# Weight sums of a fast FFN: three of four on VectorE from loaded blocks, and a later negation for the down sets

## The chip, the cores and the metric

The kernel runs on one core of one Trainium2 chip. The metric is device time in microseconds (us). Names in the profile: PE is TensorE (matmuls), PEld its weight loads, DVE is VectorE, ACT is ScalarE, POOL is GpSimd, SP is SyncE; a "q" behind a name (SPq, POOLq) is the engine's sequencer, which issues DMAs and waits.

## The reference, cut to what matters

The network is a trunk of two layers on 528 tokens (512 and 16 learned ones) with a width of 1024. Each layer is FFN, token mixer, FFN; the mixer is not touched here. All values are float32.

```python
def swiglu(x, w_gate, w_up, w_down):
    return (jax.nn.silu(x @ w_gate) * (x @ w_up)) @ w_down

for l in range(DEPTH):                      # DEPTH = 2
    h = h + 0.5 * swiglu(rmsnorm(h, norm_gains[l, 0]), ffn_w_gate[l, 0], ffn_w_up[l, 0], ffn_w_down[l, 0])
    h = h + mixer(rmsnorm(h, norm_gains[l, 1]), ...)
    h = h + 0.5 * swiglu(rmsnorm(h, norm_gains[l, 2]), ffn_w_gate[l, 1], ffn_w_up[l, 1], ffn_w_down[l, 1])
return rmsnorm(h, final_norm)[:, N_META:]
```

The four FFNs have a hidden width of 2816. Of the last one only 512 of the 528 tokens are needed.

## The kernel before, in words

**Seven products in place of eight.** A product of two matrices, each cut into 2 x 2 blocks, is made with seven block products instead of eight (Strassen's scheme in Winograd's form). The weights of a "set" are four blocks W11, W12, W21, W22 of 128 x 1024 floats (512 KB) in DRAM (`win`). Three products use a block as it is: "1" takes W11, "2" takes W12, "4" takes W22. The other four need sums of blocks:

- "7": S3 = W21 - W11
- "6": S2 = W22 + S3
- "5": S1 = W21 + W22
- "3": S4 = S2 - W12

An FFN has 15 sets: 11 pairs for gate and up (sets 0 to 10, each making 256 hidden columns of both), in groups of 4, 4 and 3, and four down sets (11 to 14, two behind each of the first two groups). The down product of the third group is made in the plain way. From one pair to the next the order of products interleaves: 1 of the next pair, 7 of this one, 2 of the next, 4 and 3 of this one, 6 and 5 of the next (`ffn_steps`). Behind a group of four its two down sets are worked off, and products 1, 2, 6, 5 of the next pair stand among their last products.

**hi and lo.** The weights go to PE in two parts: `hi`, a cast that ACT makes (L264), and `lo`, the rest, that DVE makes by subtracting `hi` (L265). A product is 24 matmuls of 264 columns (256 in the last FFN), about 2.9 us of PE. `make` runs three products ahead of use, `fetch` nine; `hi` and `lo` have four buffers each, and a cast waits until PE is done with the block four places before. Casts are queued behind the last snapshot (`W.behind`).

**Snapshots.** Products 1, 6 and 7 leave an intermediate state of a PSUM accumulator, which ACT copies out (L575, `c<-ss`), before the next product may add to that accumulator. Other PSUM reads are on DVE (L581, L591, L598 in the pairs, L693 in the down sets, where `h` is added to). In the down sets ACT and DVE also make the operands (L646, L647, L651).

**The weight sums.** `block` (L198) loads a block of `win` by SP's queue. `negative` (L203) is a copy with factor -1 on ACT, in the profile `s<-w`. `add` (L208) is a DMA of POOL's queue that adds to what is in the tile. Before the change a set gets:

- S3: negation of W11 (ACT), then the accumulating load of W21 from DRAM (POOL, `s<-win`)
- S2: load of W22 (SP), then the accumulating copy of S3 (POOL, `w<-s`)
- S1: load of W21 (SP), then the accumulating load of W22 (POOL, `w<-win`)
- S4: for pairs 0 and 1 the negation of W12 and an accumulating copy of S2 (`s<-w`); from set 2 on a subtraction on DVE (L233, `s<-w,w`), when the block of product 6 has been cast

All but S4 are traced in `fetch`, at the moment when block W11 is requested (in the opening two pairs of the first FFN, in `make`).

**Buffers.** Raw blocks have 3 buffers (`wraw`), S3 and S4 share 3 (`wsa`), S2 and S1 share 3 (`wsb`). A buffer is reused when its readers are done, so an instruction that writes it may wait in its queue.

**Order.** Each engine and each DMA queue works in order. The order is written by a planner at build time: it goes by the position in the program and by a model of when operands and buffers will be there. So an instruction whose data come later than modelled holds up what stands behind it in its queue.

## Time and profile before

| what | value |
|---|---|
| median of 3 runs | 2238.69 us (2238.67 to 2239.18) |
| profiled execution | 2233.24 us, of which span 2231.4 us |
| PE busy, weight loads busy | 2170.3 us (97%), 2075.3 us (93%) |
| DVE busy | 1700.7 us (76%) |
| ACT busy | 1244.2 us (56%) |
| POOL | 164.4 us (7%), nearly all of it the issue of 188 DMAs |
| granted PE clock, mean | 0.996 |
| DMA | 330.29 MB, mean 148 GB/s |

The four FFNs lie at about 7 to 370, 775 to 1130, 1130 to 1480 and 1860 to 2210 us of the span (a first product may start before the last down product of the FFN ahead ends); the mixers lie between. Rows are read like this: a group of instructions has line, engine, operation, out<-in by the program's names with the numbers left off, count, then busy time, mean ns of one, and idle time of the engine before them with what ended it. A wait row has engine, tile and line of who waits, then who ended the wait, then us in total, times, longest. A timeline row has start, duration, engine, line, operation, and in brackets the idle time before it and what ended that. The tile `w` is any block of `win`, `s` is S3 or S4, `ss` is PSUM.

### The profile page before, as it was taken

To read this page: it belongs to the slowest core of one execution; us is meant where nothing else is said; L and a number is where in the kernel's file an instruction comes from. 1 tells how busy PE (TensorE), PEld (TensorE's weight loads), DVE (VectorE), ACT (ScalarE), POOL (GpSimd) and SP (SyncE) were. 2 spreads that over 40 slices of the span, in tenths; PEclk is the share of its full clock that TensorE was granted. 3 is DMA by queue.
4 is the path that set the end of the run, shared out by engine and by line. 5 is a ranking of instruction groups with operands and counts; after the bars stand their busy time and mean duration, and the time that the engine had idled before them with its cause. 6 is when DMAs were issued, how large, how long until landed. Compare 5 with 4: busy or idle time off the path is not lost. (4 is left out here: it accounts for less than half of the span.)

```text
span 2231.4 us, 40120 instructions
## 1 busy us (share of the span) xinstructions
PE 2170.3 (97%) x16506; PEld 2075.3 (93%) x16506; DVE 1700.7 (76%) x2623; ACT 1244.2 (56%) x1815; POOL 164.4 (7%) x192
## 2 busy tenths in 40 slices
PE   7999999999999999999999999999999999999898
PEld 7999999989999999999999999999788888999897
DVE  8877877577876679687788778676779768687777
ACT  8555555345784555454675455553557836545553
POOL 1111100000000011111011111000000001111100
PEclk9999999999999999999999999999999999999999
DMA  9877753212114577777668777421111237677761
GB/s 280 226 190 203 198 150 109 77 48 72 43 39 133 133 189 191 211 203 190 179 166 212 190 208 202 139 100 67 57 67 57 88 104 199 177 200 191 187 180 67
DMA packets 92647, 330.29 MB, mean 148 GB/s; under 512 B 10288, under 2 KB 12720, under 8 KB 92464
## 3 DMA queue, kind: packets, MB, share of 16 engines
q1 hardware_dynamic: 63440, 226.65, 28.2%
q0 software_dynamic: 27072, 98.58, 24.4%
q8 instruction: 130, 2.13, 0.4%
q10 hardware_dynamic: 1952, 2.50, 0.4%
q14 instruction: 53, 0.43, 0.1%
HBM read 289.94 MB, written 2.10 MB: 131 GB/s over the span
## 5 line engine op out<-in xcount | busy, mean ns | idle before, releaser
L571 PE MATMUL ss<-xc,whi 128*128 128x264 f32 (+1 forms) x4928 | 909.2, 286 | 26.1 <-ACT c L575 16.5
L571 PEld LDWEIGHTS ss<-xc,whi 128*128 128x128 f32 x4928 | 768.8, 190 | 31.1 <-ACT c L575 18.8
L571 PE MATMUL ss<-xc,wlo 128*128 128x264 f32 (+1 forms) x2464 | 702.8, 285 | 2.7 <-DVE wlo L265 2.7
L265 DVE TENSOR_TENSOR wlo<-w,whi 128x1024 fp32r<-128x1024 f32 (+1 forms) x301 | 365.3, 1216 | 152.8 <-ACT whi L264 152.7
L571 PEld LDWEIGHTS ss<-xc,wlo 128*128 128x128 f32 x2464 | 467.4, 190 | 4.3 <-DVE wlo L265 4.3
L264 ACT CAST whi<-w 128x1024 fp32r<-128x1024 f32 (+1 forms) x301 | 312.1, 1048 | 136.2 <-PE ss L571 52.2
L438 PE MATMUL mm<-x,whi 128*128 128x264 f32 (+1 forms) x1712 | 384.8, 315 | 0.0
L438 PEld LDWEIGHTS mm<-x,whi 128*128 128x128 f32 x1712 | 278.4, 188 | 16.6 <-issue 1.0
L438 PE MATMUL mm<-x,wlo 128*128 128x264 f32 (+1 forms) x856 | 266.1, 315 | 0.0
L685 PE MATMUL ss<-g,whi 128*128 128x264 f32 (+1 forms) x1280 | 239.5, 285 | 4.4 <-DVE h L693 3.1
L264 ACT CAST whi<-raw 128x1024 fp32r<-128x1024 f32 x126 | 132.0, 1048 | 163.6 <-PE mm L438 102.8
L685 PEld LDWEIGHTS ss<-g,whi 128*128 128x128 f32 x1280 | 198.6, 188 | 7.0 <-ACT whi L264 3.4
L265 DVE TENSOR_TENSOR wlo<-raw,whi 128x1024 fp32r<-128x1024 f32 x126 | 153.9, 1221 | 59.3 <-ACT whi L264 58.4
L685 PE MATMUL ss<-g,wlo 128*128 128x264 f32 (+1 forms) x640 | 181.2, 283 | 0.0
L575 ACT COPY c<-ss 128x528 f32<-128x528 f32 (+1 forms) x132 | 78.3, 593 | 181.6 <-PE ss L571 181.4
L265 DVE TENSOR_TENSOR wlo<-s,whi 128x1024 fp32r<-128x1024 f32 x120 | 146.5, 1221 | 37.5 <-ACT whi L264 37.5
L438 PEld LDWEIGHTS mm<-x,wlo 128*128 128x128 f32 x856 | 159.6, 188 | 8.5 <-issue 0.7
L438 PE MATMUL ss<-g,whi 128*128 128x264 f32 (+2 forms) x900 | 166.2, 299 | 0.0
L438 PEld LDWEIGHTS ss<-g,whi 128*128 128x128 f32 x900 | 131.7, 188 | 5.3
L264 ACT CAST whi<-s 128x1024 fp32r<-128x1024 f32 x120 | 126.1, 1051 | 10.9 <-PE ss L571 7.2
L208 POOL DMA_DIRECT2D w<-win x60 | 54.5, 908 | 1029.3 <-DVE wlo L265 410.3
L203 ACT ACTIVATE s<-w 128x1024 f32<-128x1024 f32 x68 | 71.6, 1056 | 89.7 <-DMA w<-win 77.9
(265 smaller groups left out, 3405.4 us busy)
## 6 DMA issues: line engine op xcount, KB each, us to landing
w<-win SPq DMA_DIRECT2D x299, 512.0 KB, 5.4
raw<-wts SPq DMA_DIRECT2D x126, 512.0 KB, 3.2
s<-win POOLq DMA_DIRECT2D x60, 512.0 KB, 5.2
w<-s POOLq DMA_DIRECT2D x60, 512.0 KB, 5.5
w<-win POOLq DMA_DIRECT2D x60, 512.0 KB, 7.5
s<-w POOLq DMA_DIRECT2D x8, 512.0 KB, 8.4
h<-xt SPq DMA_DIRECT2D x3, 528.0 KB, 6.3
out<-h ACTq DMA_DIRECT2D x4, 256.0 KB, 2.4
```

What stands on the lines that cost most here:

```text
L203: self.nc.scalar.activation(t, w, AF.Copy, scale=-1.0)
L208: self.nc.gpsimd.dma_start(t, src, accum_op=ALU.add)
L264: nc.scalar.copy(hi[:, cs], w[:, cs])
L265: nc.vector.tensor_tensor(lo[:, cs], w[:, cs], hi[:, cs].bitcast(F32), ALU.subtract)
L438: TE.matmul(acc.half[i][:width], lhs, rhs[:, acc.spans[i]], start=first, stop=last)
L571: TE.matmul(acc[:, j], a[:, j, k], b[:, at], start=bool(begin and k == 0 and i == 0), stop=k == len(x) - 1 and i == 2, skip_group_check=no ...
L575: W.behind = S.copy(part(st, q), acc).ins
L685: TE.matmul(acc[:, j], a[:, j, k], xs[b][:, k], start=bool(begin and k == 0 and i == 0), stop=k == 3 and i == 2, skip_group_check=not begin)
```

## The change

For pairs 2 to 10 of every FFN (36 sets) S3, S2 and S4 are made on DVE:

- `fetch` loads W21 by SP into the buffer of S3 and W22 into the buffer of S2; there is no negation and no accumulating DMA for them
- when W11 has been cast (product 1), DVE makes S3 = W21 - W11 in place
- when W12 has been cast (product 2), DVE makes S2 = W22 + S3 in place
- S4 is made as before, when product 6 has been cast
- S1 stays a load and an accumulating DMA

For the down sets (11 to 14, 16 sets) the sums stay with ACT's negation and POOL's DMAs, but negation, accumulating load and accumulating copy are traced in `make`, behind the cast of W11, instead of in `fetch`. Their loads of W22 and the sum S1 stay in `fetch`. Pairs 0 and 1 are as before.

```diff
-    def sums(self, f, i, product, w):
+    def begin_sums(self, f, i, w=None):
         got = self.summed
-        if product == "1":
+        s3 = None
+        if i < 2:
             s3 = self.negative(f, i, "s3", w)
             self.add(s3, self.dram(f, i, "21"))
-            s2 = self.block(f, i, "22", self.short, "wsb")
+        elif i < NPAIR:
+            s3 = self.block(f, i, "21", self.long, "wsa")
+        s2 = self.block(f, i, "22", self.short, "wsb")
+        if i < 2:
             self.add(s2, s3)
-            got[f, i, "7"], got[f, i, "6"] = s3, s2
-        if product == "12"[(f, i) in OPENING]:
-            s1 = self.block(f, i, "21", self.short, "wsb")
-            self.add(s1, self.dram(f, i, "22"))
-            got[f, i, "5"] = s1
...
+        got[f, i, "7"], got[f, i, "6"] = s3, s2
+        if (f, i) not in OPENING:
+            self.first_sum(f, i)
+
+    def first_sum(self, f, i):
+        s1 = self.block(f, i, "21", self.short, "wsb")
+        self.add(s1, self.dram(f, i, "22"))
+        self.summed[f, i, "5"] = s1
+
+    def sums(self, f, i, product, w):
+        got, V = self.summed, self.nc.vector
+        if (f, i) in OPENING and product in "12":
+            (self.begin_sums if product == "1" else self.first_sum)(f, i, *[w] * (product == "1"))
+        if i < 2:
...
+        elif product == "1":
+            if i < NPAIR:
+                V.tensor_tensor(got[f, i, "7"], got[f, i, "7"], w, ALU.subtract)
+            else:
+                got[f, i, "7"] = self.negative(f, i, "s3", w)
+                self.add(got[f, i, "7"], self.dram(f, i, "21"))
+            if not i < NPAIR:
+                self.add(got[f, i, "6"], got[f, i, "7"])
+        elif product == "2":
             self.kept = w
-        if product == "6" and late:
+            if i < NPAIR:
+                V.tensor_tensor(got[f, i, "6"], got[f, i, "6"], got[f, i, "7"], ALU.add)
+        elif product == "6":
             s4 = self.long.tile([P, SLAB], F32, tag="wsa", name=f"s4_{f[0]}{f[1]}_{i}")
-            self.nc.vector.tensor_tensor(s4, w, self.kept, ALU.subtract)
+            V.tensor_tensor(s4, w, self.kept, ALU.subtract)
             got[f, i, "3"] = s4
@@ def fetch
                 if load[2] == "1" and load[:2] not in OPENING:
-                    self.sums(*load, self.raws[self.fetched])
+                    self.begin_sums(*load[:2], self.raws[self.fetched])
@@ def make
-            if not isinstance(load, int) and (load[2] in "26" or load[2] == "1" and load[:2] in OPENING):
+            if not isinstance(load, int) and load[2] in "126":
                 self.sums(*load, w)
```

More of the change, by code (lines that the diff above doesn't have):

```diff
@@ L218, in sums @@
             self.add(s2, s3)
-            got[f, i, "7"], got[f, i, "6"] = s3, s2
-        if product == "12"[(f, i) in OPENING]:
-            s1 = self.block(f, i, "21", self.short, "wsb")
-            self.add(s1, self.dram(f, i, "22"))
-            got[f, i, "5"] = s1
-        late = 2 <= i
-        if product == "2" and not late:
-            s4 = self.negative(f, i, "s4", w)
-            self.add(s4, got[f, i, "6"])
-            got[f, i, "3"] = s4
-        if product == "2" and late:
+        got[f, i, "7"], got[f, i, "6"] = s3, s2
@@ new lines, in begin_sums @@
+        if (f, i) not in OPENING:
[9 more added lines that the diff above has]
+        if i < 2:
+            if product == "2":
+                s4 = self.negative(f, i, "s4", w)
+                self.add(s4, got[f, i, "6"])
+                got[f, i, "3"] = s4
+        elif product == "1":
[7 more added lines that the diff above has]
+        elif product == "2":
```

## The prediction, made before the changed kernel was run

> **What bounds the kernel now.** I read the page first: busy time of the engines, then what TensorE (PE) waited for over the whole run.

> ```profile
> span 2231.4 us, 40120 instructions
> PE 2170.3 (97%) x16506; PEld 2075.3 (93%) x16506; DVE 1700.7 (76%) x2623; ACT 1244.2 (56%) x1815; POOL 164.4 (7%) x192
> ```

> PE is busy 97% of the span, so everything that helpers save can bring at most the 61 us in which PE stands. The question is which stand ends because of the code that changes. The waits of PE, longest in total first (us, times, longest):

> ```profile
> PE ss L571 <- ACT c L575: 16.5, 11, 4.8
> PE ss L685 <- DVE c L647: 9.4, 14, 0.9
> ...
> PE ss L685 <- DVE h L693: 3.1, 2, 1.6
> ```

> The first row is the largest: products wait for a snapshot (L575) that ACT copies out of PSUM. Asked by stretch, 11.2 of its 16.5 us lie in the last FFN (1840 to 2200 us, first row below), 2.5 in the second (760 to 1100), 1.0 in the first after its start (48 to 350):

> ```profile
> PE ss L571 <- ACT c L575: 11.2, 3, 4.8
> ...
> PE ss L571 <- ACT c L575: 2.5, 3, 1.5
> ...
> PE ss L571 <- ACT c L575: 1.0, 2, 0.5
> ```

> So an ordinary change from pairs to down sets costs 0.5 us here (two in the first FFN, two of the second's three), and two in the last FFN cost 4.8 each; what is left is 1.5 in the second FFN and 11.2 - 2 x 4.8 = 1.6 in the last. ACT's timeline across one of these, and PE's row behind it:

> ```profile
> 1934.86 1.05 ACT L264 CAST whi<-w 128x1024 fp32r<-128x1024 f32 x1
> 1935.81 0.83 ACT L646 CAST g<-g 128x768 fp32r<-128x768 f32 x1
> 1942.97 1.06 ACT L203 ACTIVATE s<-w 128x1024 f32<-128x1024 f32 x1 [6.33 <-DMA w<-win]
> 1943.93 0.81 ACT L646 CAST c<-g 128x768 fp32r<-128x768 f32 x1
> 1944.66 0.58 ACT L575 COPY c<-ss 128x512 f32<-128x512 f32 x1
> ...
> 1945.29 0.50 PE L571 MATMUL ss<-xc,whi 128*128 128x256 f32 x2 [4.84 <-ACT c L575]
> ```

> This carries the prediction. The negation (L203) of down set 12 stands in ACT's queue ahead of the snapshot and waits 6.33 us for its block W11 to land; the snapshot, ready long before, stands behind it, and PE waits 4.84 us. The same comes again at 2076 us with set 14. All negations together:

> ```profile
> L203 ACT ACTIVATE s<-w x68: 1039/1058/1066, 7.6 to 2141.6; 128x1024 f32<-128x1024 f32 x68
> ...
>   DMA w<-win: 77.9, 18
>   DVE wlo L265: 11.7, 15
> ```

> ACT stood 89.6 us before negations; nearly all of it is hidden, because PE has casts made three products ahead. Where it is not hidden it is the row above.

> **The change part by part, and the sum**, against the profiled execution's 2233.24 us (span 2231.4), which is 5.45 us under the median of 2238.69; I carry the difference over to the median.

> *Pairs 2 to 10 (9 in each of 4 FFNs, 36 sets).* Per set one negation, one accumulating load s<-win and one accumulating copy w<-s go; a plain load on SP and two VectorE (DVE) sums come. Rows that price them:

> ```profile
> L203 ACT ACTIVATE s<-w 128x1024 f32<-128x1024 f32 x68 | 71.6, 1056 | 89.7 <-DMA w<-win 77.9 <-DVE wlo L265 11.7
> L233 DVE TENSOR_TENSOR s<-w,w 128x1024 f32<-128x1024 f32 x52 | 63.4, 1219 | 0.1
> ...
> w<-win SPq DMA_DIRECT2D x299, 512.0 KB, 5.4
> ...
> s<-win POOLq DMA_DIRECT2D x60, 512.0 KB, 5.2
> w<-s POOLq DMA_DIRECT2D x60, 512.0 KB, 5.5
> w<-win POOLq DMA_DIRECT2D x60, 512.0 KB, 7.5
> ```

> ACT loses 36 x 1.056 = 38 us, DVE gains 72 x 1.219 = 88 us (the fourth sum, L233, is the very same operation). POOL issues 72 DMAs fewer, SP 36 more; the copies w<-s (36 x 0.5 MB) vanish from the DMA engines. What covers the 88 us is idle DVE beside a busy PE:

> ```profile
> core 0: us, PE busy (x) PEld busy (x) DVE busy (x) ACT busy (x) POOL busy (x), PEclk, DMA share, GB/s
> ...
> 1946.00:1950.00 4.00, 4.00 (x24) 4.00 (x24) 2.99 (x5) 1.25 (x3) 0.00 (x0) 0.61 0.72 134
> 1966.00:1970.00 4.00, 4.00 (x21) 4.00 (x22) 3.93 (x4) 0.00 (x0) 0.00 (x0) 0.57 0.02 4
> 2076.00:2083.00 7.00, 6.57 (x33) 6.58 (x34) 4.65 (x7) 3.48 (x5) 1.31 (x2) 0.55 0.52 95
> ...
> 855.00:895.00 40.00, 38.65 (x308) 37.71 (x307) 37.48 (x45) 20.94 (x24) 4.35 (x5) 1.00 0.73 196
> ...
> 900.00:975.00 75.00, 75.00 (x616) 75.00 (x616) 50.74 (x63) 36.68 (x44) 8.66 (x11) 1.00 0.73 196
> ```

> From 900 to 975 us (pairs 5 to 7) PE is full and DVE busy 50.7 of 75; three to four sets add at most 9.8, so cost nothing. If that cover goes, it is at the eight changes into down sets, where DVE has 37.5 of 40 us. There the sums of pair 4 (pair 8) fall behind the worst: DVE answered the cast of 870.35 only at 877.67, but had 2.42 us idle before 896.96, just where these two sums (2.44 us) come.

> ```profile
> 870.35 1.05 ACT L264 CAST whi<-s 128x1024 fp32r<-128x1024 f32 x1 [0.15 <-ACT whi L264]
> ...
> 877.67 1.22 DVE L265 TENSOR_TENSOR wlo<-s,whi 128x1024 fp32r<-128x1024 f32 x1
> ...
> 896.96 1.22 DVE L265 TENSOR_TENSOR wlo<-s,whi 128x1024 fp32r<-128x1024 f32 x1 [2.42 <-ACT whi L264]
> ```

> Between 0 and 2.44 us each, 0 to 20 in all; nearest is the idle 2.42, so I take 0.25 each: +2.

> *Added waits.* The first new sum waits in DVE's queue for the block W21; behind it stand the next lo subtractions and the PSUM adds, and PE needs these. That load takes the slot which the negation took before, but no longer waits for W11, a negation and a POOL issue, so it lands earlier than the accumulate that it replaces. On SP it stands ahead of W22 and W21 of the same set and of the next raw blocks; if its slot is late, these are. No row shows that wait: from below nothing, from above one load, 5.4 us, in DVE's queue, against casts that run three products (8.8 us) ahead. I take 0 in the sum and keep the upper end for a rival. Block W11 is held one sum (1.2 us) longer, which the same lead covers.

> *Down sets (4 per FFN, 16).* The negation moves from the block's arrival to behind the cast of product 1; two POOL DMAs follow it there. So it waits for no block any more. What is late next is sum S2, needed by the cast of product 6. In the second FFN:

> ```profile
> 851.73 1.05 ACT L264 CAST whi<-w 128x1024 fp32r<-128x1024 f32 x1
> 853.93 0.60 ACT L575 COPY c<-ss 128x528 f32<-128x528 f32 x1 [1.14 <-PE ss L571]
> ...
> 857.83 1.06 ACT L203 ACTIVATE s<-w 128x1024 f32<-128x1024 f32 x1 [2.36 <-DMA w<-win]
> ...
> 859.29 0.86 POOL L208 DMA_DIRECT2D s<-win  x1 [9.14 <-ACT s L203]
> 864.77 0.86 POOL L208 DMA_DIRECT2D w<-s  x1 [4.61 <-DMA s<-win]
> ...
> 868.20 2.00 ACT L264 CAST whi<-w 128x1024 fp32r<-128x1024 f32 x2
> ```

> Counted in program order, the cast at 851.73 is product 1 of set 11 and the one at 868.20 its product 6. A negation at 852.78 fits the 1.14 us that ACT stands idle before the snapshot. From negation to landing: 1.46 to the first POOL issue, 5.48 to the second, 5.5 to land, 12.4 us: 865.2, 3 us early. With 7.5 per landing, the slowest kind of POOL DMA above, it is 16.5: 869.3, 1.1 us late. So 0 to 1.1 at eight first sets; I take 0.25 each, +2, nearest the measured chain. The second sets have 17 us or more.

> *What goes.* (a) The two 4.84 and 4.8 us stands shrink to the ordinary 0.5: -8.6. (b) The granted clock behind them is about half, above: (1-0.61)x4 + (1-0.57)x4 + (1-0.55)x7 = 6.4 us lost, and at the other changes, with stands of 0.5 and 0.9, it stays 1.00: -6.4. (c) The waits on L693, 3.1 us in two, come only in the last FFN, in the crowd after the block; 0.4 each remains: -2.3. (d) In two FFNs pair 2's negation waits for a buffer, with a snapshot behind it, and PE stands 1.5 and 1.6 us at this place:

> ```profile
> 1882.60 1.06 ACT L203 ACTIVATE s<-w 128x1024 f32<-128x1024 f32 x1 [2.47 <-DVE wlo L265]
> 1883.57 0.57 ACT L575 COPY c<-ss 128x512 f32<-128x512 f32 x1
> ```

> This negation is no longer there: -2.1. Sum: -8.6 - 6.4 - 2.3 - 2.1 + 2 + 2 = -15.4.

> On (b), the row at 1966 to 1970 shows a half clock after stands of only 1.6 and 0.9 us. [...]

> **The rivals.**

> *The block only changes its name.* The planner of the order still puts something that waits for a block ahead of that snapshot, a cast of product 2, say; the stands of 4.8 us remain, and the clock with them. For: the block behind the 6.33 us was late by itself, and others are in flight. Against: casts trail their loads by more than the negations, and in the first and second FFN the same change has only 0.5. Then (d) alone is left, and +4 may eat it: 2238.7 - 2.1 + 2 = about 2238.6, no change.

> *The chain of the down sets comes late (the slower side).* Negation, two POOL DMAs, cast of product 6, all in order: S2 late by L stops ACT, then DVE, and the down sets have no slack on DVE, so PE loses about L at each of eight first sets. It takes the place of the chain's +2, so it decides from 8L = 15.4 + 2 = 17.4, L = 2.2 us. For: the margin is 3 us, POOL's queue also holds the 7.5 us sums S1, and one such in front brings L to 7.5 - 3 = 4.5, at which 8 x 4.5 - 17.4 = +18.6 gives 2257. With half the sets hit it is 18 - 17.4 = +0.6, 2239. Against: S1 of set 11 is issued at 849, before the cast.

> *DVE stands for the added block.* 5.4 us in DVE's queue less what the lead hides, seen at some changes only: at 3 us in three of eight, -15.4 + 9 = 2232.3, still a gain; it needs both more places and a half clock to be a loss.

> **How the numbers follow.** About 0.2% (4.5 us) is what a measurement of this kernel tells from no change. Forecast, with the third rival's milder gain: 0.63, at 2238.69 - 15.4 = 2223.3; no change 0.12; the slower side 0.25. The lower end is the gain without the two +2 terms, 2219.3, less an estimated 5 of the ordinary stands (9.4 us on L647 above, and the 0.5s) that ACT's freed time may shorten: 2214. The upper end is half the first sets late, 2239, and some 5 us of half clock behind their stands, as in (b): 2244. The forecast's own range is 2214 to 2233. Faster 0.63, within 0.2% 0.12, slower 0.25.

> **What would show it.** Right: no ACT wait for w<-win before L203 in the last FFN, no PE wait over 1 us at 1945 and 2076, clock 1.00 there, DVE busy about 1789 us, ACT about 1206, POOL 116 DMAs. Wrong: PE waits at the eight changes of 2 us and more, ended by a cast of w that waited for DMA w<-s, or a DVE sum that waited for w<-win.

## The result, and the profile after

The changed kernel takes 2220.39 us (median of 4 runs, 2218.53 to 2221.27) against 2238.93 us for the kernel before beside it (4 runs, 2238.67 to 2241.81): a ratio of 0.9913, 95% interval 0.9896 to 0.993. The profiled execution took 2218.53 us, 14.7 us less than that of before; the medians differ by 18.5, since the profile of before lies 5.7 us under its median and that of after 1.9. The head of its page, and then what PE waited for in the whole run:

```profile
span 2216.8 us, 40090 instructions
...
PE 2164.6 (98%) x16506; PEld 2070.7 (93%) x16506; DVE 1784.4 (80%) x2695; ACT 1210.7 (55%) x1779; POOL 101.5 (5%) x120
```

```profile
PE ss L594 <- DVE wlo L288: 8.7, 8, 3.1
PE ss L594 <- ACT whi L287: 7.6, 2, 7.4
PE ss L708 <- DVE c L670: 6.6, 8, 0.9
PE ss L594 <- ACT c L598: 6.1, 11, 0.7
```

The lines have moved by 23 (L571 of before is L594, the snapshot L575 is L598, the addition to `h` L693 is L716). The snapshots' row fell from 16.5 to 6.1 us, its longest wait from 4.8 to 0.7. The row of the `h` additions is gone. First is now a row that was small before (2.7 us, 0.7 at the longest): the `lo` subtractions of DVE, with 8.7 us and 3.1 at the longest. The second row is the start of the kernel, as before (7.3 us there). DVE gained 84 us, ACT lost 34, POOL's 120 instructions are 116 DMAs and four others.

Cut by stage (us, worked out from the two traces). A stage ends at the first addition to `h` (L537, L560 in the changed kernel) by its last products; "idle" is the time in it in which no matmul ran:

| stage | before | after | difference | idle before, after |
|---|---|---|---|---|
| first FFN | 349.4 | 357.6 | +8.2 | 16.9, 23.2 |
| first mixer | 384.3 | 384.4 | 0.0 | 3.5, 3.5 |
| second FFN | 372.2 | 369.6 | -2.6 | 5.8, 4.0 |
| third FFN | 353.0 | 351.4 | -1.6 | 5.4, 4.7 |
| second mixer | 363.8 | 363.8 | 0.0 | 2.7, 2.7 |
| last FFN | 376.2 | 357.3 | -18.9 | 17.3, 4.3 |
| end | 32.4 | 32.6 | +0.2 | 9.5, 9.7 |

So the gain lies in the last FFN, 18.9 us, and the first FFN gives 8.2 of it back. Each stage is read from one profile. Six kernels below run the first three FFNs with the very instructions of before, in the same order on each engine; with the kernel before, these seven profiles give 349.4 to 351.6 us for the first FFN, 371.7 to 373.6 for the second and 353.0 to 356.0 for the third. The profile of before is at the low end in the first and the third. Against these seven the first FFN loses 6 to 8 us, and the second and third together gain about 4 to 9, which is part of why the medians differ by more than the profiles.

ACT's timeline across the change to the down sets in the last FFN, the place where it stood 6.33 us before:

```profile
1941.52 0.58 ACT L598 COPY c<-ss 128x512 f32<-128x512 f32 x1 [1.30 <-PE ss L594]
1942.00 1.06 ACT L287 CAST whi<-s 128x1024 fp32r<-128x1024 f32 x1
1942.95 1.05 ACT L287 CAST whi<-w 128x1024 fp32r<-128x1024 f32 x1
1944.66 1.06 ACT L203 ACTIVATE s<-w 128x1024 f32<-128x1024 f32 x1 [0.66 <-DMA w<-win]
```

The negation of set 12 now stands three places behind the snapshot, which waits only for PE. The negation still waits for its block, 0.66 us, and nobody waits for that. The loss in the first FFN: what DVE waited for between 40 and 130 us, then its timeline, then PE's row behind it:

```profile
DVE w L244 <- DMA w<-win: 6.6, 2, 5.0
```

```profile
64.35 1.22 DVE L244 TENSOR_TENSOR w<-w,w 128x1024 f32<-128x1024 f32 x1 [4.98 <-DMA w<-win]
65.50 0.77 DVE L648 TENSOR_TENSOR g<-c 128x264 f32<-128x264 f32 x2
66.18 1.22 DVE L288 TENSOR_TENSOR wlo<-w,whi 128x1024 fp32r<-128x1024 f32 x1
...
67.46 0.39 PE L594 MATMUL ss<-xc,wlo 128*128 128x264 f32 x1 [3.13 <-DVE wlo L288]
```

The new sum S3 (L244) stands in DVE's queue and waits 4.98 us for the added block W21. The `lo` that PE needs stands behind it, and PE stands 3.13 us. It is the very form of the fault that left ACT's queue: an instruction that waits for a load, ahead of one that PE waits for. In the whole run 16 of the 36 sums S3 wait so:

```profile
DVE w L244 <- DMA w<-win: 33.4, 16, 5.1
```

Four of the others are as long (3.5 to 5.1 us, at 194, 948, 1299 and 2027 us), and PE has no stand behind them. Why the two at the start of the first FFN are not covered was not shown.

### The profile page after: what moved, and what is told of

It reads as the page before. It is cut to its first block, busy times and chain, and to the rows that moved or that the text cites. A ratio compares the mean times of both kernels' runs of the same rounds, so it can differ in the third digit from the quotient of the medians.

```text
span 2216.8 us, 40090 instructions
## 1 busy us (share of the span) xinstructions
PE 2164.6 (98%) x16506; PEld 2070.7 (93%) x16506; DVE 1784.4 (80%) x2695; ACT 1210.7 (55%) x1779; POOL 101.5 (5%) x120
## 4 chain that ended last, share of the span: by engine, by line
PE 79%; DVE 11%; ACT 3%; issue 2%; DMA 1%; DVEq 0%; POOL 0%; ACTq 0%; POOLq 0%
PE ss L594 36%; PE mm L461 13%; PE ss L708 11%; PE ss L461 10%; PE sm L461 2%; DVE wlo L288 2%; DVE g L674 1%; PE sm L1069 1%; PE ss L1044 1%; DVE h L716 1%; PE ss L467 1%; DMA w<-win 1%; PE sm L1085 1%; ACT t L440 1%; DVE c L670 1%
## 5 line engine op out<-in xcount | busy, mean ns | idle before, releaser
L594 PE MATMUL ss<-xc,whi 128*128 128x264 f32 (+1 forms) x4928 | 905.3, 285 | 15.6 <-ACT whi L287 7.6
L594 PEld LDWEIGHTS ss<-xc,whi 128*128 128x128 f32 x4928 | 765.3, 189 | 20.5 <-ACT c L598 8.4
L594 PE MATMUL ss<-xc,wlo 128*128 128x264 f32 (+1 forms) x2464 | 701.5, 285 | 8.8 <-DVE wlo L288 8.7
L594 PEld LDWEIGHTS ss<-xc,wlo 128*128 128x128 f32 x2464 | 465.4, 189 | 11.2 <-DVE wlo L288 11.0
L288 DVE TENSOR_TENSOR wlo<-w,whi 128x1024 fp32r<-128x1024 f32 (+1 forms) x337 | 408.0, 1217 | 64.1 <-ACT whi L287 63.9
L287 ACT CAST whi<-w 128x1024 fp32r<-128x1024 f32 (+1 forms) x337 | 349.4, 1048 | 175.2 <-PE ss L594 82.1
L598 ACT COPY c<-ss 128x528 f32<-128x528 f32 (+1 forms) x132 | 78.4, 594 | 259.1 <-PE ss L594 259.1
L208 POOL DMA_DIRECT2D w<-win x60 | 52.8, 880 | 1580.1 <-DVE wlo L288 463.9
L708 PEld LDWEIGHTS ss<-g,wlo 128*128 128x128 f32 x640 | 120.9, 189 | 0.0
L440 ACT ACTIVATE c<-c 128x528 f32<-128x528 f32 (+1 forms) x88 | 56.5, 642 | 93.6 <-DVE c L638 89.3
L708 PE MATMUL ss<-c,whi 128*128 128x264 f32 (+1 forms) x512 | 100.3, 289 | 7.1 <-DVE c L670 6.6
## 6 DMA issues: line engine op xcount, KB each, us to landing
w<-win SPq DMA_DIRECT2D x335, 512.0 KB, 4.5
raw<-wts SPq DMA_DIRECT2D x126, 512.0 KB, 3.3
w<-win POOLq DMA_DIRECT2D x60, 512.0 KB, 7.5
s<-win POOLq DMA_DIRECT2D x24, 512.0 KB, 7.0
w<-s POOLq DMA_DIRECT2D x24, 512.0 KB, 5.6
s<-w POOLq DMA_DIRECT2D x8, 512.0 KB, 7.7
```

What stands on the lines that cost most here:

```text
L208: self.nc.gpsimd.dma_start(t, src, accum_op=ALU.add)
L287: nc.scalar.copy(hi[:, cs], w[:, cs])
L288: nc.vector.tensor_tensor(lo[:, cs], w[:, cs], hi[:, cs].bitcast(F32), ALU.subtract)
L440: prev_act[0] = S.activation(*args, **kw).ins
L594: TE.matmul(acc[:, j], a[:, j, k], b[:, at], start=bool(begin and k == 0 and i == 0), stop=k == len(x) - 1 and i == 2, skip_group_check=no ...
L598: W.behind = S.copy(part(st, q), acc).ins
```

## The experiments

The edits are cut to what matters, some of them put in words. Each ratio is to runs of the kernel before that were taken beside that run; their medians lie between 2236.97 and 2239.71 us.

**The two halves.** The pairs' sums alone (down sets as before), and the down sets alone (pairs as before):

```diff
 pairs alone, from the changed kernel
-        if i < 2:
+        if i < 2 or i >= NPAIR:      # negation and both additions in fetch
 down sets alone, from the changed kernel
-        if i < 2:
+        if i < NPAIR:
-            V.tensor_tensor(S3 ...), V.tensor_tensor(S2 ...)
```

> Part one alone: sums S3 and S2 of pairs 2 to 10 on DVE; the down sets' negation where it was, when the block is requested. Theory (the last FFN's two stands of 4.8 us and the half clock behind them come from the down sets' negation in ACT's queue): the two stands stay, within a microsecond, the last FFN keeps 370 us or more of its 376, and what is gained is pair 2's 0.9 us in two FFNs less the first FFN's loss of up to 8: 2236 to 2246. Rival (the gain comes from the 36 negations and 72 accumulating DMAs that pairs lose, which free ACT, POOL and the DMA engines): most of the gain is here, 2218 to 2226.

> Part two alone: the down sets' negation behind the cast of W11; pairs 2 to 10 as before, with negations and accumulating DMAs. Theory: the last FFN loses its 17 to 19 us as in the changed kernel, the first FFN keeps its 349 us, pair 2's stands of 1.5 and 1.6 stay: 2218 to 2223, as fast as the whole change or a little faster. Rival (pairs carry the gain): 2236 to 2240.

The pairs alone took 2245.88 us, ratio 1.0032 (1.0021 to 1.0044); the down sets alone 2212.73 us, ratio 0.9884 (0.987 to 0.9899). Waits of PE in the last FFN, pairs alone and then down sets alone:

```profile
PE ss L589 <- ACT c L593: 11.2, 3, 5.5
PE ss L703 <- DVE h L711: 3.1, 2, 1.6
```

```profile
PE ss L588 <- ACT c L592: 2.6, 3, 1.6
PE ss L702 <- DVE c L664: 1.9, 3, 0.9
```

The pairs alone came out as the theory said; the down sets alone came out 5 us under the range that was expected of them. The whole gain is the down sets', and they do better alone than in the whole change. The pairs' part costs: its first FFN takes 360.1 us against 349.4. The 1.6 us that the down sets leave at a snapshot is pair 2's negation, which only the pairs' part removes (0.7 us is left at that place with the pairs alone).

**The wait of DVE.** The changed kernel, with S3 queued behind `lo` of product 1:

```diff
-                V.tensor_tensor(got[f, i, "7"], got[f, i, "7"], w, ALU.subtract)
+                with self.tc.issue_after(self.last_lo):
+                    V.tensor_tensor(got[f, i, "7"], got[f, i, "7"], w, ALU.subtract)
```

> The changed kernel with one thing more: S3's new sum is queued on DVE behind the lo subtraction of product 1, so that it can no longer stand in DVE's queue ahead of other lo subtractions while its block W21 is in flight. Theory (the first FFN lost 8.2 us because DVE stood 1.6 and 5.0 us before these sums, with the lo parts that PE needed behind them): the PE waits for wlo between 50 and 75 us (1.3, 3.1 and 1.4 us) and the half clock at 121 us go, the first FFN ends at 350 to 353 us in place of 357.6, and the time is 5 to 8 us under the changed kernel's 2220.4: 2212 to 2216. Rival (the loss is the amount of DVE work, 2.44 us more for each set, or the DMA engines' fullness at the start): the order changes nothing, 2219 to 2222.

2213.78 us, ratio 0.9888 (0.9871 to 0.9904). DVE no longer waits for `w<-win`, the first FFN takes 353.1 us instead of 357.6, and the other stages stay within 0.3 us. The theory held for the three waits for `lo`: they are gone, and that FFN has 5.2 us less of idle PE; one more half clock, at 41 us, takes an estimated 1.7 of it back (mean granted clock of the profile 0.997, of the change's 0.998). What is left, 3.7 us over the profile of before, is mostly that half clock and the first change into down sets, where PE stands 0.97 and 1.41 us (0.90 before) and a half clock follows at 116 us. The changed kernel has the same stand, and ACT shows what is late:

```profile
112.58 1.05 ACT L287 CAST whi<-w 128x1024 fp32r<-128x1024 f32 x1 [4.45 <-DMA w<-win]
...
119.79 0.86 PE L708 MATMUL ss<-g,whi 128*128 128x264 f32 x2 [1.41 <-ACT g L669]
```

This cast is product 5 of set 11, and it waits for sum S1. POOL issues S1's accumulating load at 102.42 us, behind S2's accumulating copy of the same set, and it lands 10.1 us later; in the kernel before it landed 7.6 us after its issue. The SiLU and the casts of the down operands stand behind the cast. With S3 behind `lo` the load lands at 108.03 us and the cast starts at 108.13. No run moved this load.

**Which part of the down sets' move counts.** First, in the kernel before, only the negations of sets 12 and 14 of the last FFN, traced behind the cast of their block:

```diff
-            s3 = self.negative(f, i, "s3", w)           # all sets, in fetch
+            if not ((f, i) in (((1, 1), 12), ((1, 1), 14))):
+                s3 = self.negative(f, i, "s3", w)       # these two: in make, behind the cast of "1"
```

> The kernel before with the negation of only two sets, 12 and 14 of the last FFN, moved behind the cast of their W11. Theory (these two negations, waiting 6.3 us each for their block ahead of a snapshot, make the whole of the last FFN's loss): the last FFN falls from 376 to about 358 us, the time to 2219 to 2224, with everything else as before. Rival (the loss of the last FFN is spread over its sets, or another wait takes the place): a gain of 5 us or less, 2233 to 2239.

2239.95 us, ratio 1.0003 (0.9993 to 1.0012): nothing. ACT's timeline shows why:

```profile
1948.57 1.06 ACT L203 ACTIVATE s<-w 128x1024 f32<-128x1024 f32 x1 [6.67 <-DMA w<-win]
1949.53 0.81 ACT L658 CAST c<-g 128x768 fp32r<-128x768 f32 x1
1950.25 0.58 ACT L587 COPY c<-ss 128x512 f32<-128x512 f32 x1
```

The negation reads the loaded block and not its cast. Being traced behind the cast doesn't tie it to the cast, and the planner left it where it was. So I tied it:

```diff
+            with self.tc.issue_after(self.behind):       # the last snapshot
+                s3 = self.negative(f, i, "s3", w)
```

> The kernel before with the negations of sets 12 and 14 of the last FFN, and no others, tied behind the snapshot ahead of which they stood in ACT's queue. (Moving them in the program alone, in the run before, left them at the same place in the queue, since a negation reads only the loaded block, and the two stands stayed.) Theory (these two places in one queue make the last FFN's loss): stands of 0.5 us in place of 4.8, no half clock behind them, last FFN 357 to 360 us in place of 376, time 2213 to 2222. Rival (the ACT wait is only the last of several that end together, so another ends there): 2233 to 2240.

2228.6 us, ratio 0.995 (0.9938 to 0.9963), between theory and rival. Waits of PE in the last FFN:

```profile
PE ss L698 <- DVE h L706: 3.1, 2, 1.6
PE ss L584 <- ACT c L588: 2.0, 3, 1.6
```

The two stands of 4.8 us are gone and the last FFN went from 376.2 to 367.0 us, 9.1 less. The two waits for `h` stayed, so they don't come of the late block. There are 13.7 us of half clock as before (0.50 granted, here from 1965.9 to 1972.7 us for one), but at another place: the two stretches right behind the stands are gone, and those behind the waits for `h` grew from 3.4 to 13.7 us.

The other way round, the four down sets of the last FFN as the change has them, untied, and everything else as before:

```diff
-                s3 = self.negative(f, i, "s3", w)       # sets 11 to 14 of the last FFN: not in fetch
+            if product == "1" and f == (1, 1) and NPAIR <= i:
+                self.sums(*load, w, cast=True)          # but in make, behind the cast of "1"
```

> The kernel before with the negation and the two accumulating DMAs traced behind the cast for the four down sets of the last FFN alone (three FFNs and all pairs as before). Theory (the gain of the change lies in the last FFN, where the planner then turns both orders, that of ACT and that of PE): the last FFN at 357-360 us, the stages ahead of it as in the kernel before, time 2217-2223. Rival (the down sets of the other three FFNs gain too, as the median of the run with all 16, 2212.7, suggests): the same last FFN, but some 8 us less than that run gained; both give about 2220, and the stages tell them apart: with the rival FFN 2 and 3 take 2 to 3 us more here than in the run with all 16, in the profile of either.

2218.59 us, ratio 0.9917 (0.99 to 0.9933), as much as the whole change. The last FFN takes 358.2 us, without a half clock (mean granted clock of the profile 0.998, in the kernel before 0.996). The second and third FFN take 1.4 and 2.4 us more than with all 16 sets, the first 2.7. The theory held for the last FFN. The rival has some truth too: the other down sets are worth some 6 us by these stages, and 5.9 by the medians.

**What the last 9 us are.** The compiled order differs between the last two kernels, though ACT has the same two casts between snapshot and negation in both. PE's blocks at the first of the two changes, with the number of matmuls in brackets (D1 is product 1 of down set 11, D1' of set 12, P7 product 7 of the pair; the kernel before has the first row too, the changed one the second):

```
tied negations:   P7(24) D1(18) P4(24) P3(24) D2(18) D5(18) D1(6) D1'(1) D2(1) D1'(3) D2(5) D1'(2) D5(1) D1'(18) D5(5)
last FFN's sets:  P7(24) D1(2) P4(24) D1(16) P3(24) D2(18) D5(18) D1(6) D2(6) D5(6) D1'(24)
```

In the first row D1' lies in pieces among the last quarters of D2 and D5, so that several results come due together. I forced PE's order in two steps in the last FFN, the first step with and without the tied negations, both steps with them:

```diff
+            with after(last matmul of D5 if this is D1' else None):      # first step
+            with after(last matmul of P4 if this is D1 else None):       # second step, added
                 TE.matmul(...)
```

> The kernel before with that order of PE's matmuls alone; the two negations stay ahead of the snapshots. Theory (two causes that add up: late blocks ahead of the snapshot, and the order of the matmuls): two stands of 4.8 us at the snapshots remain, the waits of 1.5 us and over for h go, and the last FFN comes from 376 to 365-370 us, time 2227-2233. Rival (the waits for h are the crowd after the late block): the last FFN stays at 374-377, time 2236-2241.

> The kernel before with the negations of sets 12 and 14 of the last FFN behind the snapshot (as in the run before), and with one thing more: the first product of the second down set of a group of the last FFN is queued on PE behind the last quarter of product 5 of the first set, as it stands in the changed kernel, where before it lies in pieces between those quarters. Theory (the waits of 1.6 us for h and the half clock of 6.8 us behind them come from the order of PE's matmuls at the change, where the results of two products come due together, and not from a late block): the waits for h and the half clocks at 1966 and 2092 us go, the last FFN comes from 367 to 357-360 us, time 2216-2222. Rival (they belong to the order of casts on ACT and sums on DVE, which this kernel leaves as before): the last FFN stays at 365-369 and the time at 2226-2231.

> The kernel of the second order run (negations of sets 12 and 14 behind the snapshot, first product of the second set behind the quarters of the first) with one tie more, again in the last FFN alone: the three quarters of the first set's product 1 are queued on PE behind the pair's product 4, where before they stand one product ahead of it. With that PE's order at the two changes is that of the changed kernel up to two matmuls. Theory (the 1.91 us waits for the operand of product 5 that took the place of the waits for h are the 16 to 18 matmuls, 1.9 to 2.1 us of PE, that the changed kernel holds back to this place): both waits of 1.91 us go, no half clock follows them, the last FFN comes from 362 to 357.5-359.5 us, time 2216-2221. Rival (DVE and ACT are late there by themselves, as the order of ACT's casts at the change is not that of the changed kernel): a wait of 1 to 2 us stays, the last FFN at 360-363, time 2220-2225.

The first step alone took 2236.02 us, ratio 0.9994 (0.9985 to 1.0003); with the tied negations 2223.3 us, 0.9938 (0.9923 to 0.9952); both steps with the tied negations 2226.57 us, 0.9941 (0.9925 to 0.9958). PE's waits in the last FFN, first step alone, then with the negations tied, then both steps:

```profile
PE ss L572 <- ACT c L576: 11.0, 3, 5.0
PE ss L687 <- DVE c L648: 3.7, 2, 1.9
```

```profile
PE ss L700 <- DVE c L661: 3.8, 2, 1.9
PE ss L585 <- ACT c L589: 2.0, 3, 1.6
```

```profile
PE ss L585 <- ACT c L591: 6.2, 3, 2.3
```

Each time the wait moved on: from `h` (1.6 us) to the operand of product 5 (1.9), and then to the snapshot again (2.3). The last FFN took 376.3, 362.1 and 361.7 us. For the order alone and for both steps that is what the rival expected (the time of the last, 2226.57, is 1.6 us above its range), for the middle one it lies between the two. The waits for `h` did go with the order of the matmuls, in all three, so they are of that order and not the crowd after a late block; but going, they gave little. From 367.0 to 362.1 it is the half clock that fell, from 13.7 to 3.4 us; the idle time only went from 8.3 to 7.2 us. In the last kernel ACT shows what is late:

```profile
1944.14 0.83 ACT L662 CAST c<-g 128x768 fp32r<-128x768 f32 x1 [2.62 <-DVE g L667]
1944.87 0.58 ACT L591 COPY c<-ss 128x512 f32<-128x512 f32 x1
```

The snapshot stands behind a down operand that waits for DVE's difference. In the kernel with the last FFN's sets the first operand cast comes ahead of the snapshot before it, the difference is made 4 us earlier counted from the start of the FFN (1936.2 against 1943.2 us of the span), and the snapshot stands behind nothing:

```profile
1934.33 0.84 ACT L659 CAST g<-g 128x768 fp32r<-128x768 f32 x1 [0.49 <-DVE g L638]
1935.07 0.58 ACT L588 COPY c<-ss 128x512 f32<-128x512 f32 x1
...
1940.32 0.59 ACT L588 COPY c<-ss 128x512 f32<-128x512 f32 x1 [1.30 <-PE ss L584]
```

So of the 18.0 us that the last FFN's sets bring, 9.1 are the two negations behind the snapshot. The other 8.9 came with another order of PE, ACT and DVE; most of it is the half clock, 13.7 us in the one profile and none in the other. Forcing two pieces of PE's order brought 5.3 us of it by the stages, but only 2 to 3 by the medians, and the intervals of the three ratios (0.995, 0.9938, 0.9941) overlap. Which piece of the order brings the rest stays open, and so does why the planner's order turns when all four negations are traced later.

**Negation truly behind the cast.** The changed kernel, with the 16 negations tied behind the cast of W11, or of W12:

```diff
+                with self.tc.issue_after(self.last_hi):      # made at product "1", or at "2"
                     got[f, i, "7"] = self.negative(f, i, "s3", w)
```

> The changed kernel with the 16 negations of the down sets really tied behind the cast of their W11 in ACT's queue; in the changed kernel as it is, they are traced behind it but still stand ahead of it. Chain theory (prediction: sum S2 comes 12.4 to 16.5 us after the negation against a window of 15.4, late by 0 to 1.1 us at eight first sets): the time rises by 0 to 9 us over the changed kernel's 2220.4, 2220 to 2230. Rival (casts run three products ahead, a late S2 is hidden): 2218 to 2222.

> The same with the 16 negations tied behind the cast of product 2 of their set, some 7 us later at first sets: S2 late by 4 to 8 us there, by 2 to 6 at second sets. Chain theory (PE loses about what S2 is late, L at each of eight first sets): 32 to 64 us more than the changed kernel, 2252 to 2285, with PE waiting at the eight changes. Rival (the lead of three products, 8.8 us, hides it): under 8 us more, 2218 to 2228.

2229.93 us, ratio 0.9961 (0.9946 to 0.9977), and 2339.4 us, ratio 1.0445 (1.0431 to 1.0459). Waits of PE and one of ACT behind W11, then of PE behind W12:

```profile
PE ss L709 <- ACT c L670: 3.9, 6, 0.7
PE ss L709 <- DVE g L671: 3.8, 6, 1.1
```

```profile
ACT whi L288 <- DMA w<-s: 5.6, 3, 1.9
```

```profile
PE ss L710 <- DVE g L672: 41.3, 16, 5.5
PE ss L710 <- ACT whi L289: 39.1, 8, 5.4
```

The chain of the down sets is real: one product later it stops PE at each of the eight changes, 80 us in 24 waits, and half clocks come on top (mean granted clock 0.974, in the change 0.998). That is 119 us over the change, where the theory gave 32 to 64: it counted one loss at each change, and the trace has three waits there. Behind W11 itself it costs some 10 us over the change. There S2 is late for ACT's cast three times, by 1.9 us at the longest (in the change itself never), and PE waits for the down operands; how much of these waits comes of S2, and how much of the negation itself in ACT's queue, was not separated.

**A version that takes what gains.** The first FFN's pairs as before, the other FFNs' pairs on DVE with S3 behind `lo`, the down sets as in the change:

```diff
+        old = i < 2 or f == (0, 0) and i < NPAIR      # these keep negation and accumulating DMAs
+                with self.tc.issue_after(self.last_lo):
                     V.tensor_tensor(got[f, i, "7"], got[f, i, "7"], w, ALU.subtract)
```

> Both lessons together: pairs 2 to 10 of the first FFN as before (negations and accumulating DMAs), those of the other three on DVE with S3's sum behind the lo subtraction, down sets as in the change. By stages of the profiles: first FFN 347.5 as with the down sets alone, FFNs two to four 369.5, 351.3 and 357.1 as with the sum behind lo: some 5.6 us under the latter's 2213.8, 2207 to 2210. Rival (the first FFN's loss is not of its pairs): 2212 to 2216.

2209.4 us, ratio 0.9866 (0.9853 to 0.9879), the fastest of all: 1.34% under before, and by its ratio about 0.5% under the change. Its first FFN takes 347.7 us, its last 357.2. The down sets alone, with every pair as before, had 0.9884 (0.987 to 0.9899): the intervals overlap, so the totals don't show that sums of pairs on DVE gain anything. By the stages the three later FFNs are 0.8, 1.3 and 1.1 us shorter than there.

## Why the prediction was right, and where not

The number was right: 2223.3 forecast, 2220.4 measured, and -15.4 against -14.7 between the profiled executions and -18.5 between the medians. Several terms were not.

- *(a), -8.6 for the two stands.* Right in mechanism and size: tying two negations behind the snapshots gave 9.1 us.
- *(b), -6.4 for the half clock.* Right in size: 13.7 us at a granted clock of 0.50, by estimate 6.8 us lost, are gone from the last FFN. Its cause was half of the matter. With the stands of 4.8 us gone the half clocks right behind them went, but with the `h` waits left 13.7 us remained. The bound of 61 us for all gains leaves this term out: time at half clock counts as busy (from 1966.22 us in the kernel before PE is busy for 3.41 of 3.41 us at a clock of 0.50), and PE's busy time fell by 5.7 us.
- *(c), -2.3 for the waits on L693, "in the crowd after the block".* They went altogether, -3.1, but not with the block: they stayed when the block was out of the way. Their cause is the order of the products at that place.
- *"The negation moves ... to behind the cast of product 1".* This step failed. In the order that ACT ran at the first change of the last FFN the negation of set 11 stands ahead of the cast of its block in both kernels, by seven places before and nine after. Only the negation of set 12 moved, past the snapshot. Nor is it the moved line that does it by itself: with sets 12 and 14 alone traced later nothing moved (ratio 1.0003). That the planner turns its order with all four sets was not foreseen, so this part of the gain came by luck too. "So it waits for no block any more" is wrong too; at the two changes it waits 0.66 and 0.68 us, where it harms nobody.
- *The chain of the down sets, +2, and its rival.* S2 was never late, since the negations of the first sets weren't. S1 was, at one of the eight changes: the cast that waits 4.45 us at 112.58, with the stands of 0.56 and 1.41 us and a half clock behind it. The rival spoke of S1 in front of S2 in POOL's queue; it was the other way round. Where the queue does bind the negation, S2 is late by up to 1.9 us (0 to 1.1 was the bound), and the kernel loses some 10 us in all, not all of it shown to be S2's; one product later it is 119.
- *(d), -2.1 for pair 2's negation.* Nearly right: the longest snapshot wait in the second and the last FFN went from 1.5 and 1.6 to 0.7 us, and it needs the pairs' part, as the run with the down sets alone shows.
- *DVE at eight changes, +2.* Not paid: waits on L647 (L670 now) fell from 9.4 us to 6.6.
- *The added wait for W21, taken as 0.* This is the term that was mis-sized. DVE waited 33.4 us in 16 sums, up to 5.1 us, close to the upper end of one load (5.4). The lead that the prediction counted on covered nearly all of them; at two, early in the first FFN (1.62 and 4.98 us), it did not, and PE's waits for `lo` there, 1.3, 3.1 and 1.4 us, make most of the 8.2 us that this FFN lost. The rest is the late S1 and its half clock. The third rival named this wait and priced it at 9 us, for three of eight changes; it came at the early pairs of the first FFN instead.

So the sum came out by two errors that cancel, which is luck. By FFN, with half of (d) in the second and half in the last and a quarter of each +2 in every one, the forecast was +1.0, -0.1, +1.0 and -17.4; the first came 7.2 us above it and the other three together 6.7 below. Of the signs named, these held: no PE wait over 1 us at the two changes, clock 1.00 there, DVE 1784 us against 1789, ACT 1211 against 1206, POOL 116 DMAs. "No ACT wait for w<-win before L203 in the last FFN" did not. "A DVE sum that waited for w<-win" was named as a sign of error, and it was there.

## What to carry to other kernels

An instruction that reads only a loaded block has no tie to anything but the load, so in an in-order queue an automatic order may put it ahead of work that another engine waits for: look for it by the wait for a DMA that stands directly ahead of a snapshot or a cast, and tie it behind that work, or else the fault merely changes engines, as it did here from ACT to DVE. Where code is traced is not where it runs: read the order that each queue ran before explaining a gain by the moved line. Price a change by stage, as a gain of 18.9 us and a loss of 8.2 us in different stages looked like one modest gain, and leaving out the losing stage made the fastest version measured. And see first how far the stages of kernels with the same code lie apart, 2 to 3 us here.

## What was not expected of the hardware

```profile
1962.80:1966.20 3.40, 1.07 (x4) 0.71 (x5) 3.16 (x5) 2.81 (x3) 0.00 (x0) 1.00 0.54 186
1966.20:1969.60 3.40, 3.40 (x18) 3.40 (x18) 3.40 (x4) 0.00 (x0) 0.00 (x0) 0.50 0.02 5
...
2092.50:2095.90 3.40, 1.90 (x17) 1.71 (x16) 3.40 (x6) 2.17 (x3) 0.00 (x0) 1.00 0.79 212
2095.90:2099.30 3.40, 2.17 (x14) 1.78 (x15) 3.06 (x4) 1.72 (x2) 0.00 (x0) 1.00 0.07 24
```

The kernel after, around its stand of 3.13 us and around the one of 1.41 us:

```profile
62.80:66.20 3.40, 1.53 (x13) 1.32 (x11) 1.85 (x4) 2.08 (x3) 0.00 (x0) 1.00 0.22 50
66.20:69.60 3.40, 2.14 (x17) 2.15 (x18) 3.40 (x5) 0.41 (x1) 0.00 (x0) 1.00 0.00 0
...
117.40:120.80 3.40, 1.91 (x14) 1.49 (x13) 3.20 (x7) 1.15 (x3) 0.86 (x1) 1.00 0.65 171
120.80:124.20 3.40, 3.40 (x18) 3.40 (x17) 3.40 (x5) 2.81 (x4) 0.87 (x1) 0.50 1.00 231
```

In the kernel before, the window with three short waits (PE busy 1.07 of 3.4 us) is followed by one at 0.50; in the kernel after, the stand of 3.13 us falls across two windows (PE busy 1.53 and 2.14), and the clock stays at 1.00. Of the windows of these two profiles between 24 and 2190 us that are not at half clock themselves, the three with 2.32, 2.96 and 3.41 us of idle PE were followed by half clock. Of the thirteen with 1.08 to 1.88 us one was, with 1.49 us (ahead of 120.79 us in the kernel after), and of all the others, with 0.91 us or less, none. In the run with two negations behind the snapshot a window with 1.79 us of idle PE was followed by half clock (from 1962.5 us, PE busy 1.61 of 3.4); in the one that adds the first step of PE's order, a window with 1.77 us was (from 1958.3 us) and one with 1.70 was not (from 2084.6 us). So between 1.49 and 1.88 us it went either way; what decides there was not shown. In the kernel before, the same group of waits had half clock behind it at the first change, where it fell into one window, and none at the second, where it fell into two (PE busy 1.90 and 2.17, rows above). A half clock of 3.41 us at 0.50 costs an estimated 1.7 us.
